# A hybrid encoder trunk on one core: the first two weight chunks cast on arrival and multiplied side by side, the first eight turns in eight PSUM banks, sums of squares begun at the guard value

## The chip, the cores and the metric

The kernel runs on one core of a Trainium2 chip. The metric is the device time of one execution in microseconds. The core has five engines with a queue each: TensorE (PE, matmuls and transposes; its weight loads are shown apart as PEld), VectorE (DVE), ScalarE (ACT), GpSimd (POOL), and SyncE (SP), which here only issues the transfers.

## The reference

One encoder layer, run with the same weights on two batches: a prompt of 512 tokens and a sample of 1024, 1024 channels wide.

```
h = rmsnorm(x) ; z = h @ w_in                 # 1792 columns: q 512, k 128, v 128, conv a 512, conv b 512
A = windowed attention (|q-k| <= 128, bias, sink)
B = swish(layernorm(depthwise_conv31(a * sigmoid(b))))
x = x + concat(A, B) @ w_out
u = depthwise_conv3(rmsnorm(x) @ w_up)        # 2 x 2816 columns
x = x + (silu(u[:2816]) * u[2816:]) @ w_down
y = rmsnorm(x)                                # rmsnorm(x) = x * rsqrt(mean(x*x) + 1e-6) * g
```

## The kernel before

All matmuls use pairs: a float32 operand is split into a rounded part `hi` (a cast on ScalarE, L189 for weights) and the rest `lo = x - hi` (a subtraction, on POOL at L190 for weights), and a product is `whi*hi + whi*lo + wlo*hi`, three matmuls of 128x128 by 128x512 for each of the eight blocks `kc` of the 1024 channels. In the first projection these are lines 296, 297 and 299.

**Start.** Four tiles of the prompt (128 tokens x 1024) and the first chunks of `w_in` (128 columns each) are loaded on SP's queue in this order: the four tiles, chunk 0, chunk 1, then four tiles of the sample, chunk 2. While these arrive TensorE turns the identity 36 times (L230). `make_h1(0)` norms each tile in place (`norm_in_place`): a sum of squares, on ScalarE for the even tiles (L242) and on VectorE for the odd ones (L244); on POOL `mean + EPS` (L173) and the power -1/2 (L174); on VectorE the scaling of the tile (L247). Then `transposed` makes eight turns: for each `kc` four transposes on TensorE (L255) into one PSUM bank, a scaled copy from it on ScalarE (`hi`, L257), and one op on VectorE (`lo`, L258), after which the bank is free.

`step(i, nt)` multiplies weight chunk `i` with the turned tokens `nt`. Chunk 0 is conv b, chunk 1 conv a; their results are read out by `evac`. For the first two chunks on the prompt `late_lo` puts the eight `wlo` matmuls (L303) behind the other sixteen. `want_raw` asks for a chunk's transfer, `want_w` splits it. The guard `tc.issue_after(ins)` puts what is traced within it behind `ins` on the engine of `ins`: chunk 0's cast stands behind the first turn's copy on ScalarE, chunk 1's behind the last one. `constants()` and `bias_to_dram()`, small loads, transposes and a product, are traced between steps 0 and 1. `tick()` lets convolution pieces (VectorE, with some taps on ScalarE and POOL, in PSUM bank `c0`) and side work advance between matmuls.

**Order.** The instructions of most engines are ordered by a planner, from its own idea of when each is ready; TensorE's order is written by hand from the second part of the up-projection on, SP's too in the down-projection.

**Buffers.** `Slots` hands out tiles of named sizes when the program is traced: 15 slots `q` of 4096 bytes a partition, 4 `c` of 4224, 61 `h` of 2048. It takes the first free slot of the smallest size that fits, and a slot goes back to the end of the list when the Python object that holds it is deleted (`Held.__del__`). The eight PSUM banks are handed out in the same way: `a0`, `a1`, `a2`, `u0`, `u1`, `b0`, `b1`, `c0`; `use` says which letters a job may take. A new tile in a slot waits until all readers of the slot's last tile are done, a transfer out among them. After the warm transposes the free list is `c0, u0, u1, b0, b1, a0, a1, a2`.

**End.** The sums `u`, `e`, `o11`, `o12` of the down-projection are three `q` slots each. Twelve blocks of 128 tokens are then finished by `finish(blk, parts, tail)`: two squares with sums on ScalarE (L1456), three POOL ops (L1457 to L1459) for the inverse root, the scaling of the two halves on ScalarE (L1464, L1467), POOL (L1465) and VectorE (L1469), and two transfers out (L1470). Each takes one tile `o`. For the last two blocks `left_first` does the left half's square (L1448) and its product with the norm's weights (L1449) early; the add L937 takes TensorE's last sums.

Of the kernel before, what the change touches and what calls it, by code (L numbers as in the profile page):

```python
# [29 lines left out]
EPS = 1e-6  # L30
# [112 lines left out]
def tile_hybrid_encoder(ctx: ExitStack, tc: tile.TileContext, xs, rel_bias, norm_attn_g, w_in,  # L143
                        attn_sink, conv_dw_w, conv_dw_b, conv_ln_g, conv_ln_b, w_out, norm_ffn_g,
                        w_up, ffn_dw_w, ffn_dw_b, w_down, norm_final_g, onehot, outs):
    nc = tc.nc
# [14 lines left out]
    def bank(job):  # L161
        return banks.tile([NT], among=use[job])
# [4 lines left out]
    nhalf = cst.tile([P, 1], F32, name="nhalf")  # L167
# [3 lines left out]

    def rstd_of(ss, n, out):
        nc.gpsimd.tensor_scalar(out, ss, 1.0 / n, EPS, op0=ALU.mult, op1=ALU.add)  # L173
        nc.gpsimd.tensor_tensor(out, out, nhalf[:], op=ALU.pow)  # L174

    def load_x(G, tt):
        x = sb.tile([D])
# [23 lines left out]
    raws, ws = {}, {}  # L201

    def want_raw(i):
        if i < nch and i not in raws and i not in ws:
            raws[i] = chunk_raw(w_in[0], order[i][2])

    def want_w(i):
        if i < nch and i not in ws:
            want_raw(i)
            ws[i] = split(raws.pop(i))  # L210

# [20 lines left out]
    xq = {0: [load_x(GR[0], tt) for tt in range(4)]}  # L232
    want_raw(0)
    gA, gF, cvb = vecs[:, 0:8], vecs[:, 8:16], vecs[:, 16:20]
    lng, lnb, fb = vecs[:, 20:24], vecs[:, 24:28], vecs[:, 28:72]


    def norm_in_place(x, k):
        ss, rs = sm(1), sm(1)
        junk = sb.tile([D], BF16, 2)  # L240
        if k % 2 == 0:
            nc.scalar.activation(junk[:], x[:], AF.Square, accum_out=ss[:])  # L242
        else:
            nc.vector.tensor_tensor_reduce(out=junk[:], in0=x[:], in1=x[:], scale=1.0, scalar=0.0,  # L244
                                           op0=ALU.mult, op1=ALU.add, accum_out=ss[:])
        rstd_of(ss[:], D, rs[:])
        nc.vector.tensor_scalar_mul(x[:], x[:], rs[:])  # L247

    marks = []

    def transposed(xn, g, h):
        for kc in range(KC):
            pt = bank("turn")
            for i in range(4):
                nc.tensor.transpose(pt[:, i * P:(i + 1) * P], xn[i][:, kc * P:(kc + 1) * P], ident[:])  # L255
            hi, lo = sb.tile([NT], F32R), sb.tile([NT], F32R)
            ia = nc.scalar.activation(hi[:], pt[:], AF.Identity, scale=g[:, kc:kc + 1])  # L257
            iv = nc.vector.scalar_tensor_tensor(lo[:], pt[:], g[:, kc:kc + 1], hi[:].bitcast(F32),  # L258
                                                op0=ALU.mult, op1=ALU.subtract)
            h.append((hi, lo))  # L260
            marks.append((ia.ins, iv.ins))
            yield 0.0


# [9 lines left out]
    def tick():  # L274
        pace["credit"] += pace["conv"] if convs else pace["late"]
        queue = convs or (late if pace["late"] else convs)
        while queue and pace["credit"] > 0:
            pace["credit"] -= advance(queue)
        if not queue:
            pace["credit"] = 0.0  # L280
        pace["due"] += pace["rate"]
        while side and pace["due"] >= 1.0:
            advance(side)
            pace["due"] -= 1.0
        if not side:
            pace["due"] = 0.0
# [2 lines left out]
        while queue:  # L289
            advance(queue)  # L290

    def proj(out, w, h, late_lo=False):
        whi, wlo = w
        for kc in range(KC):
            hi, lo = h[kc]
            nc.tensor.matmul(out, whi[:, kc, :], hi[:], start=(kc == 0), stop=False)  # L296
            nc.tensor.matmul(out, whi[:, kc, :], lo[:], start=False, stop=False)  # L297
            if not late_lo:
                nc.tensor.matmul(out, wlo[:, kc, :], hi[:], start=False, stop=(kc == KC - 1))  # L299
            if kc % 2 == 1 and kc < KC - 1:  # L300
                tick()
        for kc in range(KC if late_lo else 0):
            nc.tensor.matmul(out, wlo[:, kc, :], h[kc][0][:], start=False, stop=(kc == KC - 1))  # L303


    qsd = [dr.tile([4, P, NH, P], F32, name=f"qsd{i}") for i in range(3)]
# [6 lines left out]
    convs, late = deque(), deque()  # L313
# [38 lines left out]
    tanh_t, cpads, kt, vt = {}, {}, {}, {}  # L352
# [62 lines left out]
    h1 = {}  # L415

    def make_h1(nt):
        xt = xq.pop(nt)
        for k, x in enumerate(xt):
            if nt == 1:  # L420
                with tc.issue_after(marks[KC - 1][0]), tc.issue_after(marks[KC - 1][1]):
                    norm_in_place(x, k)
            else:
                norm_in_place(x, k)
            if nt:
                yield 0.0
        h1[nt] = []
        yield from transposed(xt, gA, h1[nt])

    def step(i, nt):  # L430
        kind, c, col = order[i]
        pp = bank("step")
        proj(pp[:], ws[i], h1[nt], i < 2 and nt == 0)
        evac(kind, c, nt, pp[:])
        if kind == "ca" and nt != 1:
            g = 0 if nt == 0 else 1
            (convs, late)[g].append(conv_items(g, c, cpads.pop((g, c))))
        tick()

    want_raw(1)  # L440
    for _ in make_h1(0):
        pass
    with tc.issue_after(marks[0][0]):
        want_w(0)
    xq[1] = [load_x(GR[1], i) for i in range(4)]
# [25 lines left out]
    def bias_to_dram():  # L471
        oh = sb.tile([NT])
        nc.sync.dma_start(oh[:33, :], onehot)
        rb = cst.tile([33, NH], F32, name="rb")
        nc.sync.dma_start(rb[:32, :], rel_bias)
        nc.vector.memset(rb[32:33, :], NEG)
        pbk = bank("step")
        nc.tensor.matmul(pbk[:NH, :], rb[:33, :], oh[:33, :], start=True, stop=True)
        bv = sb.tile([NT])
        nc.vector.tensor_copy(bv[:NH, :], pbk[:NH, :])  # L480
        bvd = dr.tile([NH, NT], F32, name="bvd")
        nc.sync.dma_start(bvd[:], bv[:NH, :])
        d = dr.tile([P, NH, NT], F32, name="bbd")
        nc.sync.dma_start(d[:], bvd[:].partition_broadcast(P))
        return d

    pace.update(rate=RA, conv=CA)
    for i in range(npr):
        if i == 3:
            side.append(make_h1(1))  # L490
        if i == 5:
            xq[2] = [load_x(GR[1], 4 + i) for i in range(4)]
            side.append(make_h1(2))
        if i == 1:
# [439 lines left out]
    L, R = slice(0, NT), slice(NT, W2)  # L934
# [68 lines left out]
    raws = Slots(big, {})  # L1003
# [440 lines left out]
    def left_first(tt):  # L1444

        ss, o = early[tt] = sm(2), sb.tile([D])
        part = cut(o11, tt)
        nc.scalar.activation(o[:, L], part, AF.Square, accum_out=ss[:, 0:1])  # L1448
        nc.vector.tensor_tensor(part, part, fins[0][:, L], op=ALU.mult)  # L1449

    def finish(blk, parts, tail):
        ss, o = early.pop(blk) if tail else (sm(2), sb.tile([D]))
        rs = sm(2)
        for n in range(1 if tail else 0, 2):
            s = slice(n * NT, (n + 1) * NT)
            nc.scalar.activation(o[:, s], parts[n], AF.Square, accum_out=ss[:, n:n + 1])  # L1456
        nc.gpsimd.tensor_scalar(rs[:, 0:1], ss[:, 0:1], 1.0 / D, EPS, op0=ALU.mult, op1=ALU.add)  # L1457
        nc.gpsimd.tensor_scalar(rs[:, 1:2], ss[:, 1:2], 1.0 / D, rs[:, 0:1], op0=ALU.mult, op1=ALU.add)  # L1458
        nc.gpsimd.tensor_tensor(rs[:, 1:2], rs[:, 1:2], nhalf[:], op=ALU.pow)  # L1459
        G, b = (GR[1], blk) if blk >= 0 else (GR[0], blk + 4)  # L1460
        for n in range(2):
            s = slice(n * NT, (n + 1) * NT)
            if n == 0 and not tail:
                nc.scalar.activation(o[:, s], parts[n], AF.Identity, scale=rs[:, 1:2])  # L1464
                nc.gpsimd.tensor_tensor(o[:, s], o[:, s], fins[0][:, s], op=ALU.mult)  # L1465
            elif n == 0:
                nc.scalar.activation(o[:, s], parts[n], AF.Identity, scale=rs[:, 1:2])  # L1467
            else:
                nc.vector.scalar_tensor_tensor(o[:, s], parts[n], rs[:, 1:2], fins[0][:, s], op0=ALU.mult, op1=ALU.mult)  # L1469
            nc.sync.dma_start(G["o"][b * P:(b + 1) * P, s], o[:, s])  # L1470
# [172 lines left out]
```

## Time and profile before

| | |
|---|---|
| median of three runs | 1564.2 us (1560.03, 1564.2, 1566.33) |
| the profiled execution | 1558.91 us, of it 1557.1 us span |
| TensorE busy | 97% of the span |
| VectorE, ScalarE, POOL busy | 72%, 51%, 46% |
| mean granted clock of TensorE | 0.99 |
| transfers | 227.17 MB, 146 GB/s over the span |

Times in the profile's rows are microseconds from the span's start. A row of the timeline is start, length, engine, line, operation, the tile written and those read (buffer numbers left out), the shapes, the count, and in brackets the idle time of the engine before it and who ended it. `PE u L296 <- DVE h L258` reads: TensorE's matmul of line 296, which writes a bank `u`, waited for VectorE's op of line 258, which writes an `h`.

### The profile page before, as it was taken

Reading aid. Unit: us, or ns where it says so; the run is one execution under the profiler, and the core shown is the slowest. Engines: PE = TensorE matmul, PEld = TensorE weight load, DVE = VectorE, ACT = ScalarE, POOL = GpSimd, SP = SyncE. Lnnn points to the kernel's source line nnn. Section 1 sums busy time; section 2 is a strip of 40 time slices with the busy share of each in tenths; the row PEclk is TensorE's granted clock in tenths of the full one; section 3 lists DMA queues with packets and bytes.
Section 4 is the critical chain, followed back from the end, with each engine's and each line's share of the span. In section 5 each row is a group of like instructions: output and inputs, shape, how many; then the busy total and the mean of one; then the engine's idle time right before and its main releaser. Section 6 shows DMA issues by size and latency. Waiting matters only on the chain. (4 is left out here: it accounts for less than half of the span.)

```text
span 1557.1 us, 20112 instructions
## 1 busy us (share of the span) xinstructions
PE 1506.9 (97%) x6843; PEld 1229.4 (79%) x6843; DVE 1126.2 (72%) x1604; ACT 795.4 (51%) x1404; POOL 708.9 (46%) x566
## 2 busy tenths in 40 slices
PE   8899998999999999899999999999999999999997
PEld 6787787787888888777777888888888788888885
DVE  7999767857788785344868777777776845568883
ACT  4634654335787786633454444455545543444254
POOL 7652344226666776947433455555554000003355
PEclk9999999999999999999999999999999999999999
DMA  7582334447343346779332233333331582356644
GB/s 230 156 212 81 107 100 124 129 142 217 112 132 129 118 129 181 242 238 298 114 93 76 92 104 104 105 104 102 102 115 64 200 284 82 105 165 230 221 135 162
DMA packets 228780, 227.17 MB, mean 146 GB/s; under 512 B 13268, under 2 KB 168348, under 8 KB 228549
## 3 DMA queue, kind: packets, MB, share of 16 engines
q1 hardware_dynamic: 228677, 225.88, 45.8%
q8 instruction: 54, 0.88, 0.2%
q14 instruction: 49, 0.40, 0.1%
HBM read 164.74 MB, written 62.14 MB: 146 GB/s over the span
## 5 line engine op out<-in xcount | busy, mean ns | idle before, releaser
L190 POOL TENSOR_TENSOR q<-q,q 128x1024 fp32r<-128x1024 f32 x72 | 173.4, 2415 | 93.4 <-ACT q L189 34.4
L940 POOL TENSOR_TENSOR q<-q,q 128x512 fp32r<-128x512 f32 x101 | 140.0, 1391 | 164.0 <-ACT q L1050 151.7
L940 DVE TENSOR_TENSOR h<-h,h 128x512 fp32r<-128x512 f32 (+2 forms) x202 | 153.9, 794 | 65.2 <-ACT h L944 25.3
L1398 PE MATMUL w<-h,h 128*128 128x512 f32 x462 | 181.4, 393 | 1.4 <-DVE q L1185 1.4
L1399 PE MATMUL w<-h,h 128*128 128x512 f32 x462 | 181.5, 393 | 0.0
L1400 PE MATMUL w<-h,h 128*128 128x512 f32 x462 | 181.1, 392 | 0.0
L1064 PE MATMUL w<-h,q 128*128 128x512 f32 x448 | 176.5, 394 | 1.0 <-ACT h L1147 0.6
L1066 PE MATMUL w<-h,q 128*128 128x512 f32 x448 | 175.5, 392 | 1.0 <-POOL q L940 1.0
L1065 PE MATMUL w<-h,q 128*128 128x512 f32 x426 | 166.4, 391 | 0.0
L296 PE MATMUL u<-h,q 128*128 128x512 f32 x400 | 161.0, 403 | 5.4 <-DVE h L837 4.1
L297 PE MATMUL u<-h,q 128*128 128x512 f32 x400 | 158.6, 397 | 0.0
L299 PE MATMUL u<-h,q 128*128 128x512 f32 x384 | 151.8, 395 | 2.7 <-POOL q L190 2.7
L937 POOL TENSOR_TENSOR q<-q,q 128x1024 f32<-128x1024 f32 x12 | 32.4, 2707 | 236.6 <-DVE q L937 220.0
L339 DVE SCALAR_TENSOR_TENSOR c<-c,cvw,c 128x512 f32<-128x512 f32 x184 | 138.0, 750 | 2.9
L944 ACT CAST h<-h 128x512 fp32r<-128x512 f32 x120 | 71.9, 619 | 93.2 <-DVE h L940 41.9
L296 PE MATMUL b<-h,q 128*128 128x512 f32 x256 | 102.7, 401 | 3.3 <-DVE d L369 2.2
L1398 PEld LDWEIGHTS w<-h,h 128*128 128x128 f32 x462 | 86.8, 188 | 21.6 <-ACT h L944 1.8
L1400 PEld LDWEIGHTS w<-h,h 128*128 128x128 f32 x462 | 86.7, 188 | 19.7
L1399 PEld LDWEIGHTS w<-h,h 128*128 128x128 f32 x462 | 86.8, 188 | 19.5
L837 DVE SCALAR_TENSOR_TENSOR h<-u,fw,h 128x511 f32<-128x511 f32 x88 | 65.5, 744 | 49.8 <-ACT h L841 49.0
L299 PE MATMUL b<-h,q 128*128 128x512 f32 x256 | 101.4, 396 | 0.0
L297 PE MATMUL b<-h,q 128*128 128x512 f32 x256 | 101.1, 395 | 0.0
(417 smaller groups left out, 3670.4 us busy)
## 6 DMA issues: line engine op xcount, KB each, us to landing
q<-in_w_up SPq DMA_DIRECT2D x88, 512.0 KB
ga<-q SPq DMA_DIRECT2D x64, 256.0 KB
h<-ga SPq DMA_DIRECT2D x57, 256.0 KB
q<-in_w_in SPq DMA_DIRECT2D x28, 512.0 KB
h<-in_w_down SPq DMA_DIRECT2D x52, 256.0 KB
q<-in_x_sample SPq DMA_DIRECT2D x15, 512.0 KB
h<-qsd SPq DMA_DIRECT2D x24, 256.0 KB
x1d<-q SPq DMA_DIRECT2D x11, 512.0 KB
```

Source lines behind the costliest of these rows:

```text
L190: (nc.vector if dve else nc.gpsimd).tensor_tensor(lo[:], raw[:], hi[:].bitcast(F32), op=ALU.subtract)
L296: nc.tensor.matmul(out, whi[:, kc, :], hi[:], start=(kc == 0), stop=False)
L297: nc.tensor.matmul(out, whi[:, kc, :], lo[:], start=False, stop=False)
L299: nc.tensor.matmul(out, wlo[:, kc, :], hi[:], start=False, stop=(kc == KC - 1))
L339: nc.vector.scalar_tensor_tensor(acc[:], src(t), w(t), acc[:], op0=ALU.mult, op1=ALU.add)
L940: (eng or nc.vector).tensor_tensor(out, a, b, op=ALU.subtract)
L1064: nc.tensor.matmul(out, whi[:, s], hi[:], start=(start and c == 0), stop=False, **go)
L1065: nc.tensor.matmul(out, whi[:, s], lo[:], start=False, stop=False, **go)
L1066: nc.tensor.matmul(out, wlo[:, s], hi[:], start=False, stop=(stop and c == 3), **go)
L1398: nc.tensor.matmul(out, sh[:, c], th[:], start=(p == 0), stop=False)
L1399: nc.tensor.matmul(out, sh[:, c], tl[:], start=False, stop=False)
L1400: nc.tensor.matmul(out, sl[:, c], th[:], start=False, stop=(p == NPAIR - 1))
```

## The change

- Chunks 0 and 1 are cast on ScalarE without a guard, traced ahead of the turns; their two subtractions on POOL stand behind the power of the fourth norm.
- `first_two` replaces steps 0 and 1 on the prompt: for each `kc` the `whi` matmuls of both chunks, in two banks, then the eight `wlo` matmuls of the one and of the other. `late_lo` goes. The constants and the bias are traced after both.
- For the first eight turns the bank `c0` is allowed too.
- A norm's sum on VectorE starts at EPS with the scale 1/1024, and its POOL op L173 goes; in `finish` the squares are scaled by 1024 to the power -1/2, and two POOL ops become one.
- `want_raw` remembers which chunks it has asked for; `marks` holds the powers of the norms, `last` the turns.

```diff
     def rstd_of(ss, n, out):
         nc.gpsimd.tensor_scalar(out, ss, 1.0 / n, EPS, op0=ALU.mult, op1=ALU.add)
-        nc.gpsimd.tensor_tensor(out, out, nhalf[:], op=ALU.pow)
+        return nc.gpsimd.tensor_tensor(out, out, nhalf[:], op=ALU.pow)
...
     def want_raw(i):
-        if i < nch and i not in raws and i not in ws:
+        if i < nch and i not in raws and i not in ws and i not in asked:
+            asked.add(i)
             raws[i] = chunk_raw(w_in[0], order[i][2])
 
     def want_w(i):
-        if i < nch and i not in ws:
+        if 1 < i < nch and i not in ws:
...
+    marks = []
+
     def norm_in_place(x, k):
...
-            nc.vector.tensor_tensor_reduce(out=junk[:], in0=x[:], in1=x[:], scale=1.0, scalar=0.0,
+            nc.vector.tensor_tensor_reduce(out=junk[:], in0=x[:], in1=x[:], scale=1.0 / D, scalar=EPS,
                                            op0=ALU.mult, op1=ALU.add, accum_out=ss[:])
-        rstd_of(ss[:], D, rs[:])
+        if k % 2 == 0:
+            root = rstd_of(ss[:], D, rs[:])
+        else:
+            root = nc.gpsimd.tensor_tensor(rs[:], ss[:], nhalf[:], op=ALU.pow)
+        marks.append(root.ins)
         nc.vector.tensor_scalar_mul(x[:], x[:], rs[:])
...
+    def first_two():
+        pp = [bank("step") for _ in range(2)]
+        for kc in range(KC):
+            hi, lo = h1[0][kc]
+            for i in range(2):
+                whi = ws[i][0]
+                nc.tensor.matmul(pp[i][:], whi[:, kc, :], hi[:], start=(kc == 0), stop=False)
+                nc.tensor.matmul(pp[i][:], whi[:, kc, :], lo[:], start=False, stop=False)
+            if kc % 2 == 1:
+                tick()
+        for i in range(2):
+            for kc in range(KC):
+                nc.tensor.matmul(pp[i][:], ws[i][1][:, kc, :], h1[0][kc][0][:], start=False, stop=(kc == KC - 1))
+            kind, c, _ = order[i]
+            evac(kind, c, 0, pp[i][:])
+            pp[i] = None
+            ws.pop(i)
+            tick()
+        convs.append(conv_items(0, 0, cpads.pop((0, 0))))
+
     want_raw(1)
-    for _ in make_h1(0):
+    use.update(turn="aubc")
+    for k, x in enumerate(xq[0]):
+        norm_in_place(x, k)
+    his = []
+    for i in range(2):
+        hi = sb.tile([KC, P], F32R)
+        nc.scalar.copy(hi[:], raws[i][:])
+        his.append(hi)
+    h1[0] = []
+    for _ in transposed(xq.pop(0), gA, h1[0]):
         pass
-    with tc.issue_after(marks[0][0]):
-        want_w(0)
+    use.update(turn="aub")
+    with tc.issue_after(marks[3]):
+        for i in range(2):
+            lo = sb.tile([KC, P], F32R)
+            nc.gpsimd.tensor_tensor(lo[:], raws.pop(i)[:], his[i][:].bitcast(F32), op=ALU.subtract)
+            ws[i] = his[i], lo
+    his.clear()
+    hi = lo = None
     xq[1] = [load_x(GR[1], i) for i in range(4)]
     want_raw(2)
-    with tc.issue_after(marks[KC - 1][0]):
-        want_w(1)
...
+        if i == 0:
+            first_two()
         want_raw(i + 2)
         want_w(i + 1)
-        step(i, 0)
-        ws.pop(i)
+        if i > 1:
+            step(i, 0)
+            ws.pop(i)
...
-            nc.scalar.activation(o[:, s], parts[n], AF.Square, accum_out=ss[:, n:n + 1])
-        nc.gpsimd.tensor_scalar(rs[:, 0:1], ss[:, 0:1], 1.0 / D, EPS, op0=ALU.mult, op1=ALU.add)
-        nc.gpsimd.tensor_scalar(rs[:, 1:2], ss[:, 1:2], 1.0 / D, rs[:, 0:1], op0=ALU.mult, op1=ALU.add)
+            nc.scalar.activation(o[:, s], parts[n], AF.Square, scale=D ** -0.5, accum_out=ss[:, n:n + 1])
+        nc.gpsimd.tensor_scalar(rs[:, 1:2], ss[:, 1:2], ss[:, 0:1], EPS, op0=ALU.add, op1=ALU.add)
         nc.gpsimd.tensor_tensor(rs[:, 1:2], rs[:, 1:2], nhalf[:], op=ALU.pow)
```

More of the change, by code (lines that the diff above doesn't have):

```diff
@@ L200, in tile_hybrid_encoder @@
     nch = len(order)
-    raws, ws = {}, {}
+    raws, ws, asked = {}, {}, set()
     def want_raw(i):
-        if i < nch and i not in raws and i not in ws:
+        if i < nch and i not in raws and i not in ws and i not in asked:
+            asked.add(i)
             raws[i] = chunk_raw(w_in[0], order[i][2])
     def want_w(i):
-        if i < nch and i not in ws:
+        if 1 < i < nch and i not in ws:
             want_raw(i)
@@ L243, in norm_in_place @@
         else:
-            nc.vector.tensor_tensor_reduce(out=junk[:], in0=x[:], in1=x[:], scale=1.0, scalar=0.0,
+            nc.vector.tensor_tensor_reduce(out=junk[:], in0=x[:], in1=x[:], scale=1.0 / D, scalar=EPS,
                                            op0=ALU.mult, op1=ALU.add, accum_out=ss[:])
-        rstd_of(ss[:], D, rs[:])
+        if k % 2 == 0:
[3 more added lines that the diff above has]
+        marks.append(root.ins)
         nc.vector.tensor_scalar_mul(x[:], x[:], rs[:])
-    marks = []
+    last = []
     def transposed(xn, g, h):
@@ L260, in transposed @@
             h.append((hi, lo))
-            marks.append((ia.ins, iv.ins))
+            last.append((ia.ins, iv.ins))
             yield 0.0
@@ L290, in drain, with proj @@
             advance(queue)
-    def proj(out, w, h, late_lo=False):
+    def proj(out, w, h):
         whi, wlo = w
@@ L297, in proj @@
             nc.tensor.matmul(out, whi[:, kc, :], lo[:], start=False, stop=False)
-            if not late_lo:
-                nc.tensor.matmul(out, wlo[:, kc, :], hi[:], start=False, stop=(kc == KC - 1))
+            nc.tensor.matmul(out, wlo[:, kc, :], hi[:], start=False, stop=(kc == KC - 1))
             if kc % 2 == 1 and kc < KC - 1:
                 tick()
-        for kc in range(KC if late_lo else 0):
-            nc.tensor.matmul(out, wlo[:, kc, :], h[kc][0][:], start=False, stop=(kc == KC - 1))
     qsd = [dr.tile([4, P, NH, P], F32, name=f"qsd{i}") for i in range(3)]
@@ L420, in make_h1 @@
             if nt == 1:
-                with tc.issue_after(marks[KC - 1][0]), tc.issue_after(marks[KC - 1][1]):
+                with tc.issue_after(last[KC - 1][0]), tc.issue_after(last[KC - 1][1]):
                     norm_in_place(x, k)
@@ L432, in step @@
         pp = bank("step")
-        proj(pp[:], ws[i], h1[nt], i < 2 and nt == 0)
+        proj(pp[:], ws[i], h1[nt])
         evac(kind, c, nt, pp[:])
@@ L1447, in left_first @@
         part = cut(o11, tt)
-        nc.scalar.activation(o[:, L], part, AF.Square, accum_out=ss[:, 0:1])
+        nc.scalar.activation(o[:, L], part, AF.Square, scale=D ** -0.5, accum_out=ss[:, 0:1])
         nc.vector.tensor_tensor(part, part, fins[0][:, L], op=ALU.mult)
```

## The prediction

> **What bounds the kernel now.** I read the page's head first, then the waits of PE, then stretches of the start, then the chain that ended last.
>
> ```profile
> span 1557.1 us, 20112 instructions
> PE 1506.9 (97%) x6843; PEld 1229.4 (79%) x6843; DVE 1126.2 (72%) x1604; ACT 795.4 (51%) x1404; POOL 708.9 (46%) x566
> PE u L296 <- DVE h L837: 4.1, 2, 3.5
> PE u L687 <- DVE q L681: 4.0, 1, 4.0
> PE u L687 <- DVE h L681: 2.9, 1, 2.9
> PE u L296 <- DVE h L258: 0.9, 1, 0.9
> ```
>
> TensorE is the bound: busy 97%, and its longest waits (columns: total us, times, longest) are single waits of 3 to 4 us in stages that the edit doesn't touch. So time can be won only where TensorE stands or runs slowly, which here means the start, before the first projection, and the end, after the last matmul. The stretches of the start:
>
> ```profile
> 10.40:13.80 3.40, 1.79 (x15) 1.32 (x13) 2.05 (x4) 0.00 (x0) 2.24 (x3) 1.00 1.11 359
> 13.80:17.20 3.40, 1.62 (x12) 1.15 (x12) 1.69 (x3) 3.18 (x5) 1.48 (x1) 1.00 1.02 394
> 17.20:20.60 3.40, 3.40 (x9) 2.63 (x10) 3.40 (x6) 3.40 (x7) 0.89 (x1) 0.50 0.60 153
> 20.60:24.00 3.40, 3.40 (x16) 2.50 (x15) 3.40 (x2) 3.06 (x6) 3.21 (x2) 1.00 0.50 120
> ```
>
> Columns are length, then PE, PEld, DVE, ACT, POOL busy, then the granted clock, DMA share, GB/s. TensorE is half idle until 17.2, then full, but the first full stretch runs at a granted clock of 0.50: 9 instructions instead of 16. Who holds the start up is in the timeline:
>
> ```profile
> 12.85 0.75 DVE L247 TENSOR_SCALAR q<-q,s 128x1024 f32<-128x1024 f32 x1 [0.71 <-POOL s L174]
> 14.02 0.69 ACT L257 ACTIVATE h<-u,vecs 128x512 fp32r<-128x512 f32 x1 [5.23 <-PE u L255]
> 14.61 1.03 ACT L189 CAST q<-q 128x1024 fp32r<-128x1024 f32 x1
> 14.74 0.75 DVE L258 SCALAR_TENSOR_TENSOR h<-u,vecs,h 128x512 fp32r<-128x512 f32 x1 [1.14 <-ACT h L257]
> 15.72 2.37 POOL L190 TENSOR_TENSOR q<-q,q 128x1024 fp32r<-128x1024 f32 x1 [2.91 <-ACT q L189]
> 16.26 0.75 DVE L258 SCALAR_TENSOR_TENSOR h<-u,vecs,h 128x512 fp32r<-128x512 f32 x1 [0.77 <-ACT h L257]
> 17.07 0.70 PE L296 MATMUL u<-h,q 128*128 128x512 f32 x1 [0.87 <-DVE h L258]
> 22.84 1.99 PE L303 MATMUL u<-h,q 128*128 128x512 f32 x8
> 24.66 0.39 PE L296 MATMUL u<-h,q 128*128 128x512 f32 x1
> 31.51 0.39 PE L296 MATMUL u<-h,q 128*128 128x512 f32 x1
> ```
>
> The fourth norm ends at 13.60 (12.85 + 0.75). The first turn is copied at 14.02. The cast of chunk 0, ordered behind it, takes ScalarE from 14.61 to 15.64, so the second turn's VectorE half starts at 16.26 and ends at 17.01. Only then does its bank come free for step 0, whose first matmul starts at 17.07. Step 2 begins at 31.51. Between lie 48 matmuls at (24.66 - 22.84) / 8 = 0.2275 us = 10.9, some 1.7 us lost to the half clock (half of 3.4), and the small constant products: together nearly the whole 14.4 us. Once started, this stretch has no hole to fill.
>
> **The change part by part.** *The norms (k odd begins its sum at EPS with scale 1/D).* One POOL instruction goes in each of 6 norms.
>
> ```profile
> 5.85 0.19 POOL L173 TENSOR_SCALAR s<-s 128x1 f32<-128x1 f32 x1 [4.02 <-ACT h L242]
> 7.58 0.75 DVE L247 TENSOR_SCALAR q<-q,s 128x1024 f32<-128x1024 f32 x1 [0.44 <-POOL s L174]
> 7.63 0.75 POOL L173 TENSOR_SCALAR s<-s 128x1 f32<-128x1 f32 x1
> 8.46 0.55 POOL L174 TENSOR_TENSOR s<-s,nhalf 128x1 f32<-128x1 f32 x1
> 12.26 0.55 POOL L174 TENSOR_TENSOR s<-s,nhalf 128x1 f32<-128x1 f32 x1
> ```
>
> The tiny op costs 0.19 alone but 0.75 beside VectorE's scaling, which started 0.05 earlier at 7.58: it stands until that ends. Without it the power itself stands there and follows at once, so an odd norm gains 8.46 - 7.63 = 0.83 less the wait until 8.33, about 0.28. Two odd norms lie on this chain: 0.56, and the fourth norm ends near 13.04. Bounds: 0 (the wait merely moves to the next op) and 1.66 (both ops wholly). I take 0.56. The other four odd norms run beside projections; nothing waits for them.
>
> *The casts as they land.* ScalarE casts (1.03 each) lose their guards and stand ahead of the turns.
>
> ```profile
> 4.61 1.06 ACT L242 ACTIVATE h<-q 128x1024 bf16<-128x1024 f32 x1 [2.40 <-DMA q<-in_x_prompt]
> 7.64 1.06 ACT L242 ACTIVATE h<-q 128x1024 bf16<-128x1024 f32 x1 [1.89 <-DMA q<-in_x_prompt]
> ```
>
> Tiles 0 and 2 land at 4.61 and 7.64: 1.5 us for each 512 KB. The chunks are the next but one and the one after in the same queue, so by estimate chunk 0 lands near 10.7, chunk 1 near 12.2, and both casts end by about 13.3, in ScalarE's idle 5.23 us. Queued behind them are only the turns, whose first copy would start near 13.46. It loses nothing, and turn 1 no longer stands behind a cast. Cover gone (chunk 1 later by 1 us): the turns start 1 us late.
>
> *Eight banks.* The allocator hands out the conv bank first, then u0, u1 and so on, so the eighth turn waits for no copy. Step 0's accumulator is then u0, the second turn's, and step 1's is u1, the third's: the first matmul still waits for the second turn's VectorE half. From 13.46: copy 0.69, VectorE 0.75, VectorE 0.75 back to back, small latencies: about 15.75 against 17.07. That is the early gain, **1.3 us** (0.56 norm, 0.77 the wait on the cast). The conv bank is not used by a convolution until step 2.
>
> *Two chunks beside each other.* 32 matmuls are ready as each turn lands, then 2 x 8 with the low parts: the same 48, so only the start moves. The low parts: two POOL subtractions of 2.4 start after the fourth power (12.81 now) instead of at 15.72 and later, and are done near 18, long before the 33rd matmul. They overlap the turns' VectorE halves; the half at 16.26 took its 0.75 beside the subtraction of 15.72 as well. The constants and bias products are issued after both steps instead of between them: the same work on TensorE, the same place in SP's queue; the chunk loads keep their order (the set of asked chunks only prevents a second load). The tick count falls from 8 to 6 with one queue entry at the end: nothing waits. Cost 0.
>
> *A held buffer.* The new loop over the four prompt tiles leaves its last one bound to the name x until the function returns, so one of the 15 q slots never comes back. Its first place of need is the end. There u, e, o11, o12 hold twelve q slots and the finishing blocks turn over the rest: three now, two after.
>
> ```profile
> 1533.76 0.63 ACT L1456 ACTIVATE q<-q 128x512 f32<-128x512 f32 x1 [1.91 <-DMA out_sample<-q]
> 1542.66 0.63 ACT L1456 ACTIVATE q<-q 128x512 f32<-128x512 f32 x1 [3.33 <-DMA out_prompt<-q]
> 1545.04 0.63 ACT L1448 ACTIVATE q<-q 128x512 f32<-128x512 f32 x1 [1.04 <-DMA out_prompt<-q]
> 1546.05 0.39 PE L1400 MATMUL w<-h,h 128*128 128x512 f32 x1
> 1547.95 1.74 DVE L1469 SCALAR_TENSOR_TENSOR q<-q,s,c 128x512 f32<-128x512 f32 x1 [0.80 <-POOL s L1459]
> 1549.23 0.51 POOL L1457 TENSOR_SCALAR s<-s 128x1 f32<-128x1 f32 x1
> 1550.22 0.68 DVE L937 TENSOR_TENSOR q<-w,q 128x512 f32<-128x512 f32 x1
> 1551.82 0.26 POOL s L1458
> 1552.75 0.75 DVE q L1469
> ```
>
> Three squares wait for an output's landing. The square at 1533.76 is of a block put ahead of others on ScalarE, so the wait holds back those too. TensorE ends at 1546.44; the last add comes at 1550.22 because VectorE serves the block before it first. With two slots a block cannot be put ahead of the one two before it, which may shorten the train; but each waits for the output of that one. Bounds: -3.8 (the add right behind TensorE) and +3.0: the last block's slot is the one that the block before last wrote out; if that is as late as the output finished at 1549.69 and takes 3.6 to land (the span's rest behind 1552.75 + 0.75), the first square comes at 1553.3 and the second at 1553.9 instead of 1550.90. The rows do not say which end is nearer, since the same waits feed both; I take the middle, -0.4.
>
> *The finishing sums.* One POOL op goes per block (12) by a scale in the square. In the last block it ran at 1549.23, before the sum that it would feed at 1551.82: off the chain, 0.
>
> Sum: -1.3 - 0.4 = **-1.7 us**. The profiled execution took 1558.9 (1557.1 span and 1.8 around it) and would become 1557.2; it lies 5.3 below the runs' median of 1564.2, and to that the prediction is made: 1562.5.
>
> **The rivals.**
> *The clock does not drop (B).* The stretch 13.8 to 17.2 had PE busy 1.62 and the clock fell behind it; the one before had 1.79 and it did not. The first matmuls at 15.75 add about 1.3 us of work there, and the turns' moving earlier takes some away. If it stays up, the 1.7 us come back too: -3.4, 1560.8. The Trainium skill (TensorE: Matmul & The Clock Gate, Part 1) says that the clock drops after at least one idle window of about 3.4 us, and that the window runs free of the kernel. By that rule the clock would stay up and the time be 1560.8; the trace has a drop (0.50) after a stretch half busy, so it does not bear the rule out here.
>
> *The subtraction gets in first (E).*
>
> ```profile
> 20.71 2.40 POOL L190 TENSOR_TENSOR q<-q,q 128x1024 fp32r<-128x1024 f32 x1 [2.62 <-ACT q L189]
> 20.88 3.31 DVE L244 CUSTOM_DVE_ANT_0 h<-q 128x1024 bf16<-128x1024 f32 x1
> ```
>
> At 20.88 a VectorE op of two sources in SBUF stood behind POOL's subtraction: 3.31 us. The new subtraction follows the fourth power, as the fourth scaling does. VectorE began 0.05 ahead each time above (7.58 before 7.63); if POOL wins, the scaling stands 2.4 us and all turns with it: -1.7 + 2.4 = +0.7, 1564.9. The Trainium skill (SBUF — State Buffer, Who interferes with whom) says that VectorE and GpSimd share one port pair as an exclusive lock, and that issue order decides who stands; the trace agrees with both rows.
>
> *The two slots cost at the end (D).* +3.0 - 1.3 = +1.7: 1565.9. For it: three waits on outputs already. Against: the first of them comes from the order of the blocks, which the lost slot forbids.
>
> *The held slot starves the up-projection (C), slower.* From 850 to 1200 the weights' halves are cast and subtracted into the same q slots:
>
> ```profile
> L1050 ACT CAST q<-q x86: 607/621/627, 854.7 to 1199.4; 128x512 fp32r<-128x512 f32 x86
> L940 POOL TENSOR_TENSOR q<-q,q x86: 1285/1299/1831, 849.5 to 1198.9; 128x512 fp32r<-128x512 f32 x86
> ```
>
> With one slot fewer a cast may have to wait for the product just running. It takes 0.62 + 1.30 = 1.92 us, and a product of 12 matmuls lasts 2.7 us. It decides once a part is needed by the very next product with its queue late by over 0.8 us; then 0.6 us in each of 20 passes is +12, with the early gain +10.7: 1574.9. Against it: most parts are split two products (5.5 us) ahead.
>
> *A new order elsewhere (F).* The order on most engines is planned from the start, so shifting the start may reorder everything; if the three longest waits above (4.1, 4.0, 2.9) close, -1.7 - 11.0 = -12.7: 1551.5.
>
> **How the numbers follow.** A, the sum: 0.44; B 0.13; D 0.12; E 0.11; F 0.11; C 0.09. F alone is faster by over 0.5% (7.8 us, about what this measurement can tell), C alone slower: 0.11 and 0.09; the rest, 0.80, is the same. The range leaves F and C out: low is A with the tail's best bound and B's clock (1564.2 - 1.3 - 3.8 - 1.7 = 1557.4) less half the runs' spread (3.2), 1554; high is D and the same 3.2, 1569.1, taken as 1570.
>
> **What would show it.** First matmul of the projection near 15.75 instead of 17.07; both casts before the first turn's copy; the turns' VectorE halves without a gap; step 2 near 30.1. At the end, waits of squares on outputs of two blocks back. The prediction is wrong if the projections of weights in the later stages start to wait for casts, if the casts hold the turns, or if the waits of 3 to 4 us change.

## The result, and the profile after

| | before | after |
|---|---|---|
| median of the runs | 1563.75 us (1560.03 to 1566.33, 5 runs) | 1573.97 us (1571.19 to 1577.64, 5 runs) |
| ratio | | 1.007, 95% interval 1.0047 to 1.0093 |
| the profiled execution, its span | 1558.91, 1557.1 us | 1571.19, 1569.4 us |
| end of the last matmul to the end of the span | 10.7 us | 17.3 us |

The forecast was 1562.5 with a range from 1554 to 1570: wrong. The kernel became slower by some 10 us. In the profile the start came out as said; the end did not. In the lines of the changed kernel, L252 is the power of an odd norm, L254 a norm's scaling, L471 the casts of chunks 0 and 1, L480 their subtractions, L264 and L265 the two halves of a turn, L450 the first projection matmul. L1496 and L1488 are the squares of the finishing blocks (L1456 and L1448 before), L1504 POOL's multiplication, L1508 the last scaling, L977 the add.

The page's head, and the longest waits of PE (us in total, times, longest):

```profile
span 1569.4 us, 20126 instructions
PE 1509.5 (96%) x6843; PEld 1226.8 (78%) x6843; DVE 1135.2 (72%) x1604; ACT 794.9 (51%) x1404; POOL 711.0 (45%) x548
...
PE a L715 <- DMA h<-cvd: 5.0, 3, 3.6
PE c L751 <- DMA h<-catd: 3.2, 1, 3.2
```

POOL has 18 instructions fewer (566 to 548), as the edit says. The waits of 3 to 4 us are other ones than before but of the same size: the order in the middle did change, and gave nothing that could be told.

The start of the changed kernel, rows of the timeline:

```profile
10.86 0.85 POOL L252 TENSOR_TENSOR s<-s,nhalf 128x1 f32<-128x1 f32 x1
10.93 1.58 DVE L254 TENSOR_SCALAR q<-q,s 128x1024 f32<-128x1024 f32 x2 [0.43 <-POOL s L174]
12.67 1.05 ACT L471 CAST q<-q 128x1024 fp32r<-128x1024 f32 x1 [0.72 <-DMA q<-in_w_in]
12.66 0.27 PE L262 MATMUL c<-ident,q 128*128 128x128 f32 x1
13.62 0.68 ACT L264 ACTIVATE h<-c,vecs 128x512 fp32r<-128x512 f32 x1
14.34 0.75 DVE L265 SCALAR_TENSOR_TENSOR h<-c,vecs,h 128x512 fp32r<-128x512 f32 x1 [1.83 <-ACT h L264]
15.01 1.40 DVE L265 SCALAR_TENSOR_TENSOR h<-u,vecs,h 128x512 fp32r<-128x512 f32 x2
15.80 0.50 PE L450 MATMUL u<-h,q 128*128 128x512 f32 x1 [2.10 <-DVE h L265]
...
17.20:20.60 3.40, 3.40 (x17) 2.79 (x16) 3.40 (x5) 3.40 (x8) 1.04 (x2) 1.00 0.64 162
```

The first projection matmul starts at 15.80, forecast 15.75, and the halves on VectorE follow each other without a gap. The last row is the stretch that ran at 0.50 before: here the granted clock is 1.00. So the early gain was there in this execution, and more than the forecast.

The end of the changed kernel. First the rows of squares on ScalarE and the last matmul, then pieces of the chain that ended last (start, length, what):

```profile
1532.05 0.63 ACT L1496 ACTIVATE q<-q 128x512 f32<-128x512 f32 x1 [3.35 <-DMA out_sample<-q]
1542.31 0.63 ACT L1496 ACTIVATE q<-q 128x512 f32<-128x512 f32 x1 [5.39 <-DMA out_sample<-q]
1551.61 0.63 ACT L1496 ACTIVATE q<-q 128x512 f32<-128x512 f32 x1 [3.34 <-DMA out_prompt<-q]
1559.81 0.63 ACT L1488 ACTIVATE q<-q 128x512 f32<-128x512 f32 x1 [3.31 <-DMA out_sample<-q]
1551.70 0.40 PE L1440 MATMUL w<-h,h 128*128 128x512 f32 x1
...
1549.24 2.27 DMA out_prompt<-q
1551.61 1.34 ACT q L1496 x4
1555.71 2.94 POOL q L1504 x2
1559.09 2.26 DMA out_sample<-q
1561.46 0.46 ACT q L1488
1564.41 0.75 DVE q L1508
```

Before, the chain that ended last is traced back over one block only, from its end to the last add at 1550.29. Now it leaves TensorE at 1504.93, some 64 us before the end, and goes round: a square, a root, the scaling (on POOL or VectorE), the output's DMA (2.3 us to landing, 3.84 once), then the square of the next block in the same slot. The squares that head a round stand at 1532.05, 1542.31, 1551.61 and 1559.81, 8 to 10 us apart. TensorE is done at 1552.10, in the middle of a round, and two blocks are still to come. The sums of ScalarE's waits on outputs over the whole finishing (us in total, times, longest), before and after:

```profile
ACT q L1456 <- DMA out_prompt<-q: 8.4, 2, 5.0
ACT q L1456 <- DMA out_sample<-q: 1.9, 1, 1.9
ACT q L1448 <- DMA out_prompt<-q: 1.0, 1, 1.0
...
ACT q L1496 <- DMA out_sample<-q: 9.2, 3, 5.4
ACT q L1496 <- DMA out_prompt<-q: 7.2, 3, 3.6
ACT q L1488 <- DMA out_sample<-q: 3.6, 2, 3.3
```

11.3 us became 20.0. That made the held slot the first suspect; the experiments were to find where it costs, and what the edits are worth without it.

### The profile page after: what moved, and what is told of

Read it like the earlier page. It is cut to its first block, busy times and chain, and to the rows that moved or that the text cites. A ratio compares the mean times of both kernels' runs of the same rounds, so it can differ in the third digit from the quotient of the medians.

```text
span 1569.4 us, 20126 instructions
## 1 busy us (share of the span) xinstructions
PE 1509.5 (96%) x6843; PEld 1226.8 (78%) x6843; DVE 1135.2 (72%) x1604; ACT 794.9 (51%) x1404; POOL 711.0 (45%) x548
## 5 line engine op out<-in xcount | busy, mean ns | idle before, releaser
L190 POOL TENSOR_TENSOR q<-q,q 128x1024 fp32r<-128x1024 f32 x70 | 170.1, 2435 | 88.7 <-ACT q L189 73.6
L980 DVE TENSOR_TENSOR h<-h,h 128x512 fp32r<-128x512 f32 (+2 forms) x206 | 161.5, 817 | 65.6 <-ACT h L984 23.4
L980 POOL TENSOR_TENSOR q<-q,q 128x512 fp32r<-128x512 f32 x81 | 112.8, 1404 | 149.7 <-ACT q L1090 144.8
L303 PE MATMUL u<-h,q 128*128 128x512 f32 x384 | 154.8, 403 | 2.5 <-ACT h L264 2.5
L305 PE MATMUL u<-h,q 128*128 128x512 f32 x384 | 152.6, 397 | 0.0
L304 PE MATMUL u<-h,q 128*128 128x512 f32 x384 | 152.3, 397 | 0.0
L1104 PE MATMUL w<-h,q 128*128 128x512 f32 x368 | 145.5, 395 | 2.2 <-ACT h L1187 1.7
L1106 PE MATMUL w<-h,q 128*128 128x512 f32 x368 | 144.8, 393 | 0.6 <-POOL q L980 0.6
L977 POOL TENSOR_TENSOR q<-q,q 128x1024 f32<-128x1024 f32 x9 | 24.9, 2771 | 249.3 <-DVE q L977 232.7
L1105 PE MATMUL w<-h,q 128*128 128x512 f32 x346 | 135.5, 392 | 0.0
L980 POOL TENSOR_TENSOR c<-q,c 128x512 fp32r<-128x512 f32 x47 | 72.2, 1550 | 47.4 <-ACT c L1090 47.3
```

What stands on the lines that cost most here:

```text
L190: (nc.vector if dve else nc.gpsimd).tensor_tensor(lo[:], raw[:], hi[:].bitcast(F32), op=ALU.subtract)
L980: (eng or nc.vector).tensor_tensor(out, a, b, op=ALU.subtract)
L1104: nc.tensor.matmul(out, whi[:, s], hi[:], start=(start and c == 0), stop=False, **go)
L1105: nc.tensor.matmul(out, whi[:, s], lo[:], start=False, stop=False, **go)
L1106: nc.tensor.matmul(out, wlo[:, s], hi[:], start=False, stop=(stop and c == 3), **go)
```

## The experiments

Each ratio is against the kernel before, run on the same chip, with its 95% interval; 0.001 is 1.56 us. Times behind the last matmul are counted here from its end; the expectations count from its start, 0.4 us more.

**e1_free: the slot given back at once.**

```diff
     for k, x in enumerate(xq[0]):
         norm_in_place(x, k)
+    x = None
```

> The changed kernel with one line more, x = None behind the loop over the norms, so that the 15th q slot comes back. Theory L (the held slot is the loss, the edits themselves gain): the tail behind the last matmul goes from 17.7 us back to about 11, the middle's loss of 6 goes too, the early gain of about 3 to 6 stays; about 1560, 3 to 4 below before. Theory P (the planner's new order costs the middle, the slot only the tail): only the tail's 6.6 come back, about 1567.

Measured: 1560.55 us, ratio 0.9998 (0.998 to 1.0015). One line takes back the whole loss. What is left of the edits is -0.3 us; its interval, -3.1 to +2.3, holds the forecast early gain of 1.3 and zero as well.

**e2_before14: the kernel before with one q slot fewer.**

```diff
-    sb = Slots(big, dict(q=(15, 4096), ...
+    sb = Slots(big, dict(q=(14, 4096), ...
```

> The kernel before with 14 q slots instead of 15, nothing else. Theory L: the whole loss without the early gain, +13 to +15 against before, about 1577. Theory P: only the tail, +6 to +7, about 1570. If the slot costs nothing: within 2 us of before.

Measured: 1576.11 us, 1.0092 (1.0072 to 1.0112). The slot alone, with none of the edits, costs as much as the whole change.

**e3_late_free: the changed kernel, the slot given back behind `acc.pop`, just ahead of the finishing blocks.**

```diff
     u, e, o11, o12 = (acc.pop(n) for n in ("u", "e", "o11", "o12"))
+    x = None
```

> The changed kernel with x = None only after the last product but one, so that three q slots turn over at the end but 14 serve all before. Both theories: the tail returns from 17.7 to about 11 us and the time falls by 6 to 7, to about 1567; the middle stays as in the changed kernel. If the tail is not made by the slots, nothing changes.

Measured: 1564.84 us, 1.002 (1.0007 to 1.0033); behind the last matmul 8.9 us in place of 17.3. Most of the loss is in the finishing.

**e4_tail14: the kernel before, one free q slot struck off just ahead of the finishing blocks.**

```diff
     u, e, o11, o12 = (acc.pop(n) for n in ("u", "e", "o11", "o12"))
+    sb.free.remove(next(s for s in sb.free if s[0][0] == "q"))
```

> The kernel before with one free q slot struck off the list just ahead of the finishing blocks: two turn over instead of three, all before it is unchanged. If two slots make the tail: last matmul as before, tail 17 to 18 us instead of 11, time +6 to +7. If the tail's loss came from the changed sums of the finish: 0.

Measured: 1570.74 us, 1.0054 (1.0034 to 1.0073); behind the last matmul 18.7 us. Its last matmul ends at 1551.3, in the profile of the kernel before at 1546.4. Ahead of the finishing blocks the two are one kernel, and the distance is there long before them: by 790 us the profile before lists 3548 matmuls and e4's 3529, and 19 matmuls at 0.23 us are 4.4. So two executions of one kernel differ by some 5 us there. The changed kernel's 1552.1 is no sign of a loss ahead of the finishing, and small terms are not read from such positions.

Two differences were left for the stages ahead of the finishing: e3 less e1, 0.0022 or 3.4 us, and e2 less e4, 0.0038 or 5.9. The next two runs cut there, in the changed kernel.

**e5_free_up1 and e6_free_out: the slot given back ahead of the stage `ffn_step` (370 us), and behind it (790 us).**

```diff
+    x = None                              # e5
     pace.update(rate=RD, late=CD)
     for k in range(NJ):
...
     drain(side)
+    x = None                              # e6
```

> The changed kernel, the held slot given back ahead of the stage in which the prompt's first part of the up-projection runs beside the sample's attention (about 370 to 790 us in its trace). The tail is then that of 15 slots. Three theories on the 4.3 us that lie between returning the slot at once (ratio 0.9998) and just before the finishing (1.002). M2, the 4 us are lost in that stage, through the convolution tiles and the output weights that wait for a slot: 0.9998, about 1561, and the wait of 3 to 5 us for a convolution tile near 750 us is gone. M1, they are lost before 370 us: 1.002, about 1565. M3, lost behind 790 us, in the up-projection: 0.9998 as M2, told apart by the next run.

> The changed kernel, the held slot given back behind that stage, ahead of the rest of the up-projection (about 790 us). M2 and M1: the 4 us stay lost, 1.002, about 1565, and the wait for a convolution tile near 750 us is there as in the changed kernel. M3: 0.9998, about 1561, since the up-projection and all behind it has 15 slots.

Measured: e5 0.9999 (0.9986 to 1.0011), e6 0.9991 (0.9979 to 1.0003). M1 and M2 fall: up to 790 us fourteen slots cost nothing that could be told. M3, the stages behind 790, is what is left.

**e7_six_out: slot given back at once, and output tiles also from the three free c slots.**

```diff
+    def o_tile():
+        kind = next(s[0][0] for s in sb.free if s[1] >= 4 * D and s[0][0] in "qc")
+        return sb.tile([D], among=kind)
```

> The changed kernel with the slot given back at once and, in the finishing blocks, the three free c slots taken in turn with the three q slots, so that six output tiles turn over in place of three. Theory T, the tail's length is set by slots that wait for their output to land: the squares' waits on outputs at the end vanish and the stretch behind the last matmul, 11.2 us with three slots and 17.7 with two, falls to 8 to 9: ratio 0.998, about 1558. Rival: with three slots the tail is set by the chain of add, squares, root and scaling on VectorE, ScalarE and POOL; then six slots give no more than 0.5 us, 0.9998.

Measured: 1.0 (0.9986 to 1.0013); behind the last matmul 9.2 us, where the profiles with three slots have 8.4 to 11.1. The theory's gain did not come. The step from three slots to two costs 8 to 10 us; the step from three to six is not to be seen.

Its profile, and that of e5, showed something else. Rows of e5's start:

```profile
10.68 1.05 ACT L471 CAST q<-q 128x1024 fp32r<-128x1024 f32 x1 [1.96 <-DMA q<-in_w_in]
10.97 3.73 DVE L254 TENSOR_SCALAR q<-q,s 128x1024 f32<-128x1024 f32 x2 [0.43 <-POOL s L174]
11.81 5.10 POOL L480 TENSOR_TENSOR q<-q,q 128x1024 fp32r<-128x1024 f32 x2
17.31 0.79 PE L450 MATMUL u<-h,q 128*128 128x512 f32 x1 [1.46 <-DVE h L265]
```

Chunk 0 landed 0.2 us earlier than in the changed kernel's profile (cast at 10.68, there 10.90). POOL's subtraction started at 11.81 in place of 12.03, and the two scalings took 3.73 in place of 1.58. This is rival E, in another execution of the same start: e5 and e7 have it (casts at 10.68 and 10.55, first matmul 17.31 and 17.19), the seven profiles whose casts start at 10.90 or later do not (15.80 to 16.35).

**e8_odd_ops: slot given back at once, the odd norms' small POOL operation put back.**

> The changed kernel with the slot given back at once and the small POOL operation of the odd norms put back as it was before, nothing else. Theory: in the changed kernel the first turns' copies stand behind the cast of chunk 1 (it ends near 13.8, while the fourth norm ends near 12.5), so the norms that end earlier give nothing: the fourth norm ends 0.5 to 1.1 us later, the first copy and the first projection matmul (15.97 with the slot given back at once, counted from a cast at 12.84) stay where they are against that cast. Rival, the prediction's term: the first matmul comes 0.56 us later against that cast.

```profile
13.17 2.83 DVE L250 TENSOR_SCALAR q<-q,s 128x1024 f32<-128x1024 f32 x1 [0.71 <-POOL s L174]
13.10 5.11 POOL L477 TENSOR_TENSOR q<-q,q 128x1024 fp32r<-128x1024 f32 x2
18.75 0.79 PE L446 MATMUL u<-h,q 128*128 128x512 f32 x1 [0.73 <-DVE h L261]
```

One execution, from which no time is read. Both the theory and its rival missed. The fourth norm comes later, chunk 0 is long there, the subtraction gets in ahead of the scaling, and the first matmul starts at 18.75, 2.8 later than in e1's profile. In this profile the short norms are worth more than their own time: they win the race.

**e9_cast_dve: e7, with chunk 1 cast on VectorE, and the guard of the subtractions set to that cast.**

```diff
-        nc.scalar.copy(hi[:], raws[i][:])
+        if i == 0:
+            nc.scalar.copy(hi[:], raws[i][:])
+        else:
+            with tc.issue_after(marks[3]):              # the fourth scaling
+                marks.append(nc.vector.tensor_copy(hi[:], raws[i][:]).ins)
...
-    with tc.issue_after(marks[3]):
+    with tc.issue_after(marks[4]):
```

> The changed kernel with the slot given back at once and six output slots in the finishing blocks, and two edits at the start: chunk 1 is cast on VectorE behind the fourth norm's scaling in place of ScalarE, and both POOL subtractions stand behind that cast. Theory S: the first turn's copy no longer stands behind the cast of chunk 1 (12.67 to 13.62 in the changed kernel) and no subtraction can get in ahead of the fourth scaling (as it did where chunk 0's cast began before 10.7: two scalings of 3.60 to 3.73 and a first matmul at 17.2 to 17.3): fourth scaling ends near 12.5, first copy near 13.0, first projection matmul near 15.2 whenever the chunks land. In time 0.7 to 2 us, within what can be told: ratio 0.997 to 1.000. Rival: the cast on VectorE waits for chunk 1's landing and holds the turns as ScalarE's did: first matmul 15.8 or later, ratio 1.000.

```profile
11.03 1.58 DVE L253 TENSOR_SCALAR q<-q,s 128x1024 f32<-128x1024 f32 x2 [0.43 <-POOL s L174]
12.15 2.67 POOL L484 TENSOR_TENSOR q<-q,q 128x1024 fp32r<-128x1024 f32 x1 [0.33 <-ACT q L472]
12.80 2.57 DVE L475 CAST q<-q 128x1024 fp32r<-128x1024 f32 x1 [0.19 <-DMA q<-in_w_in]
13.07 0.69 ACT L263 ACTIVATE h<-c,vecs 128x512 fp32r<-128x512 f32 x1 [1.00 <-PE c L261]
16.74 0.51 PE L449 MATMUL u<-h,q 128*128 128x512 f32 x1 [2.94 <-DVE h L264]
```

Measured: 1559.62 us, 0.9976 (0.9961 to 0.999): 0.24% faster than the kernel before, and the only run here whose whole interval lies below 1. The mechanism expected did not work: the scalings end at 12.61 and the first copy is at 13.07 as said, but the first subtraction started at 12.15, ahead of the cast (12.80). The edit does not do what was meant: a guard orders only what stands on the engine of its instruction, here VectorE, and the subtractions stand on POOL. So the guard held nothing, and the old one behind the fourth power was gone. The cast took 2.57 us, to 15.37, and the first matmul came at 16.74. Why the kernel is faster than e7 (1.0, another chip) is open: its start in this profile is no better than an undisturbed one of the others, and its end (9.0 us) is that of e7.

**e10_hold_up2 and e11_hold_end: slot given back at once; one q slot held from 790 us to the finishing, or in the finishing alone.**

```diff
     drain(side)
+    held = sb.tile([D])                   # e10
...
     u, e, o11, o12 = (acc.pop(n) for n in ("u", "e", "o11", "o12"))
+    held = None                           # e10
+    held = sb.tile([D])                   # e11, here alone
```

> The changed kernel with the slot given back at once; one q slot is then held from the end of the sample's attention stage (about 790 us) to the last finishing block's start, and given back there. It is the lost slot in the up-projection and the down-projection alone. If those stages need the slot (M3): 3 to 4.5 us, ratio 1.002 to 1.003, POOL busy some 6 us more between 790 and 1215, and the waits at 1218 and 1225 us of 1.7 and 1.3 us in place of 0.6 and 0.5. If what the earlier pair showed (1.002 against 0.999) was the measurement's own scatter: 1.0 us, ratio 1.000.

> The changed kernel with the slot given back at once; one q slot is held in the finishing blocks alone. Theory T: the stretch behind the last matmul grows from 10.8 to 17 or 18 us, ratio 1.0045 to 1.0055, about 1569 to 1571; with the run before it, it adds to the changed kernel's 1.007. Rival, the changed kernel's long end comes from its order of the stages and not from the slot: 11 us behind the last matmul, ratio 1.000.

Measured: e10 1.0011 (0.9994 to 1.0028), e11 1.0065 (1.0041 to 1.0088); behind the last matmul 8.4 and 18.5 us. The row from 790 to 1215 us of e1, then of e10 (length, busy PE, PEld, DVE, ACT, POOL):

```profile
790.00:1215.00 425.00, 422.80 (x1867) 342.77 (x1866) 318.02 (x316) 213.34 (x318) 207.13 (x147) 1.00 0.30 96
...
790.00:1215.00 425.00, 422.93 (x1866) 342.21 (x1865) 327.42 (x316) 212.13 (x318) 214.35 (x148) 1.00 0.30 97
```

With fourteen slots VectorE and POOL are busy 9 and 7 us longer, while PE's 425 us hold the same work: the longer work is covered. The two waits that were said to grow did so, from 0.6 and 0.5 us in e1 to 2.2 and 1.3:

```profile
PE w L1106 <- ACT h L1189: 2.2, 1, 2.2
PE w L1440 <- DVE q L1227: 1.3, 1, 1.3
```

That is 2.4 us more, but other waits shrank, the one at 1229 us from 1.6 to 0.2: all waits of TensorE from 790 us on make 4.9 us in e1 and 5.7 in e10. The time's interval holds this and zero. So in the changed kernel this part is small and not settled. The 5.9 us that e2 less e4 gives for the kernel before were not cut further and stay open.

The end of e11, ScalarE's waits on outputs and the last squares:

```profile
ACT q L1497 <- DMA out_sample<-q: 9.0, 3, 5.2
ACT q L1497 <- DMA out_prompt<-q: 7.0, 3, 3.4
ACT q L1489 <- DMA out_sample<-q: 3.6, 2, 3.3
...
1545.05 0.63 ACT L1497 ACTIVATE q<-q 128x512 f32<-128x512 f32 x1 [5.22 <-DMA out_sample<-q]
1554.26 0.63 ACT L1497 ACTIVATE q<-q 128x512 f32<-128x512 f32 x1 [3.33 <-DMA out_prompt<-q]
1562.46 0.63 ACT L1489 ACTIVATE q<-q 128x512 f32<-128x512 f32 x1 [3.33 <-DMA out_sample<-q]
1552.53 0.40 PE L1441 MATMUL w<-h,h 128*128 128x512 f32 x1
```

The same rounds as in the changed kernel, 9.2 and 8.2 us apart, 19.6 us of waits: theory T, shown by the slot's absence in the finishing alone. All profiles of this case, one execution each, fall into groups by the slots that turn over in the finishing, whichever start they have:

| slots | profiles | ScalarE's waits on outputs, us | behind the last matmul, us |
|---|---|---|---|
| two | changed, e2, e4, e11, e12 | 19.6 to 20.6 | 16.8 to 18.7 |
| three | before, e1, e3, e5, e6, e8, e10 | 10.0 to 12.9 | 8.4 to 11.1 |
| six | e7, e9 | 9.5 | 9.0 to 9.2 |

**e12_after_again: the changed kernel on the same chip as e9 to e11.**

> The changed kernel itself, once more, on the same chip as the three runs before. 1.007 as before (1.005 to 1.009). If the two stages' prices add, its ratio less 1 is that of the two runs before together, to within 0.002.

Measured: 1576.59 us, 1.008 (1.0062 to 1.0098). e10 and e11 make 0.0076 together, e12 has 0.008.

## Why the prediction was wrong, step by step

*The held buffer: the step that failed.* It was seen, its place (the finishing) was right, and its price was not: -0.4, with +3.0 as the upper bound. With one slot fewer in the finishing alone the time was +10.2 us with the edits (e11: 0.0065 of 1563.9, interval 6.4 to 13.8) and +8.4 without them (e4: 0.0054 of 1561.7, 5.3 to 11.4), both against the kernel before. The upper bound took one late landing for the last block. But with two slots every pair of blocks waits for the landing of the pair ahead of it, and the delay is handed on from round to round. Three rounds of 10.3, 9.3 and 8.2 us lie between 1532.05 and 1559.81. The rows for this were there: a round is a block's own chain plus the landing, and rounds of that length can be set against the time in which TensorE finishes two blocks. The bound should have come from the ring's whole run, not from its last member. The lower bound, -3.8, was worse still: it let the slot's loss help, and by taking the middle of the two bounds the sum put the term near nothing.

*D* named the mechanism and the right sign at +3.0; *C* had the right size (+12) at the wrong place: with fourteen slots from 790 us to the finishing, the up-projection among them, the time was +1.7 us with an interval that holds zero (e10). That C's 1574.9 lies by the 1574.0 measured is chance.

*The norms.* The fourth was to end at 13.04 and ended at 12.51 (10.93 + 1.58): the norms gained 1.09 (13.60 to 12.51) where 0.56 was given.

*The casts.* They were to lose nothing and did lose some: the second started at 12.67, not at 12.2, and the first turn, whose product stood from 12.93, was copied at 13.62, behind it. Too little gain in the one term and too little loss in the other cancel, and that 15.80 comes out by 15.75 is luck.

*The race (E)* was given 0.11 and one outcome for all executions. The changed start has it in two profiles and not in seven, and what parts them is where chunk 0's cast starts: at 10.68 or before, or at 10.90 or later. Nor do starts 0.05 apart in the rows say who wins, as the prediction took them to: in the changed kernel the odd norm's power on POOL is listed at 10.86, VectorE's scaling at 10.93, and the power still stood, to 11.71. The price of 2.4 was too high: against 15.80 the first matmul came 1.4 to 1.5 late, since without it the copies stand behind the cast until 13.62 anyway.

*The clock (B).* The forecast let it drop, and in the changed kernel's profile it did not: step 2 began at 28.46 in place of 30.1. Of the thirteen other profiles, with the new start or the old, the three with the first matmul at 15.87 to 15.97 (e1, e11, e12) kept 1.00 from 17.2 to 20.6. The ten from 16.17 on ran there at 0.50 to 0.57, except e7, which kept 1.00 with 17.19. The stretch in e11 and in e10, then the first matmul of e10 and of e1:

```profile
17.20:20.60 3.40, 3.40 (x16) 2.82 (x15) 3.40 (x6) 3.40 (x8) 0.89 (x3) 1.00 0.74 193
...
17.20:20.60 3.40, 3.40 (x10) 2.67 (x9) 3.40 (x6) 3.40 (x7) 0.83 (x3) 0.56 0.63 163
...
16.17 0.50 PE L450 MATMUL u<-h,q 128*128 128x512 f32 x1 [2.16 <-DVE h L265]
15.97 0.51 PE L450 MATMUL u<-h,q 128*128 128x512 f32 x1 [2.18 <-DVE h L265]
```

So B, too, seems to be an event of the execution. Where the clock stayed up, the changed kernel and e12 began step 2 at 28.46 and 28.48; where it fell, e3 and e6 began it at 30.51 and 30.60: about the 1.7 us said, and the 0.5 by which their first matmul was later. But the gain need not arrive. In e1 and e11 the clock stayed up too, and step 2 began at 30.43 and 30.25, no earlier than in e10 (30.38), where it fell:

```profile
30.43 0.50 PE L303 MATMUL u<-h,q 128*128 128x512 f32 x1 [1.78 <-ACT h L364]
```

The bank that step 2 needs is read out by ScalarE (L364), and in e1 that stood behind two weight casts which waited for a load until 27.89; in the changed kernel it stood behind one, begun at 25.39. The prediction saw no such wait. Nor did it have what decides the clock: it counted on more work of TensorE in the stretch 13.8 to 17.2, and e1 kept the clock with 1.23 us busy there where e10, with 1.24, and the kernel before, with 1.62, lost it. The Trainium skill's rule on the clock (TensorE: Matmul & The Clock Gate, Part 1), by which the drop comes after an idle window of about 3.4 us, is not borne out by TensorE's idle time: in e10 its last idle time before its first matmul was 2.16 us, and the clock fell; in e1 it was 2.18, and it did not. That this window runs free of the kernel, which the prediction cites from the Trainium skill too, would fit an outcome that changes from one execution to the next; no run here shows where a window lay.

*F.* The order in the middle changed, the long waits moved, as the prediction named for a sign of being wrong, and e1, e5 and e6 show no gain or loss from it that could be told. *The finishing sums* at 0 agree with e1 within its interval; no run tells them alone.

## What to carry to other kernels

A name that outlives its loop can hold a buffer: when an edit takes one slot from a ring, find the stage where the ring is smallest, and price it as the round (a block's own chain plus the landing of its output) against the time the producer gives it, over all rounds, not as one late landing at the end. Where two engines race for the same moment within 0.2 us, or a clock decision lies as near, the outcome belongs to the execution: price it as a mean, and if the order matters fix it, with a guard on the engine that is to wait. Sum waits over the same work and not over the same times: one wait of 5.0 us ends at 1520.58 in the kernel before and at 1527.33 in e1, so a sum begun at 1525 us holds it in the one and not in the other. One profile's positions here moved by 5 us with nothing changed ahead of them; pairs of kernels that hold a resource in one stage alone, timed side by side, found what positions could not.

## What the runs showed of the hardware that was not expected

A cast of 128x1024 on VectorE, begun 0.65 us behind POOL's subtraction, took 2.57 us (e9) and ended at 15.37, 0.55 behind the subtraction's end at 14.82; a scaling of that size that begins first takes 0.75. One of the two stands, and who comes first may turn on 0.2 us of a transfer's landing. The clock fell with TensorE idle for 2.16 us (e10) and stayed up with 2.18 (e1), and their busy time in the stretch before was 1.24 and 1.23 us, so neither decides it alone. A 256 KB output took 2.26 to 2.39 us from its issue to its landing at the end of the kernel, and 3.84 in one round; a ring of two pays that each time. The stretch from 1525 us on moved 119 GB/s, where the start moved 394, so it was not short of bandwidth. The odd norm's power, a 128x1 operation on POOL, took 0.85 beside VectorE's scaling; the same operation takes 0.55 in other rows.
